# A Fourier and Hyena encoder layer on one core: the filter taps' first operations ordered behind the Fourier copies, and six second weight parts made by a GpSimd subtraction

## The chip, the cores and the metric

The kernel runs on one core of one Trainium2 chip. A core has a matrix engine (TensorE, PE in the profile, with its weight loads as PEld), VectorE (DVE), ScalarE (ACT), GpSimd (POOL) and SyncE (SP, which here only issues transfers), each with its own in-order stream of instructions, and 16 DMA engines that all queues share. The metric is the device time in microseconds of one execution, and less is better. The time of the kernel before is the median of three runs, 2421.94 us (2418.77 to 2423.49).

## What is computed

Two sequences of 1024 positions and 1024 channels go through the same layer in float32. Cut to what matters:

```python
xn = rmsnorm(x, g_pre)
p = xn @ w_in                                   # 1024 x 8192
fv, fg, hv, hg, mg = split(p)                   # 1, 1, 3, 1, 2 times 1024 columns
fz = fft2(fv in 4 groups of 256 channels).real  # over positions and a group's channels
y_f = (fz * silu(fg)) @ w_fourier_out
v, x1, x2 = split(short_conv(hv, w_short))      # width 3 along the positions
kf = hyena_filters(...)                         # rfft of filters made by a small sine network
z = v
for n, gate in enumerate((x1, x2)):
    z = gate * long_conv(z, kf[:, n], hyena_d[n])
y_h = (z * silu(hg)) @ w_hyena_out
g_f, g_h = split(sigmoid(mg + b_merge))
out = (g_f * y_f + g_h * y_h) @ w_out
return x + rmsnorm(out, g_post)
```

A filter is the product of a sine network's output (`hid` here) with a third weight matrix, times an exponential decay, divided by the sum of its absolute values. These products are called taps below.

## The kernel before

Nearly every product is made from two parts: a number is rounded to a first part h, and the rest is the second part l, so that h + l is the number. A product of two numbers is then three matmuls (h h, h l, l h; `mm3`). A helper, `split`, makes the parts: ScalarE casts to h, and an engine that is named subtracts h from the number, which gives l.

The kernel has three stages. **`phase_fourier`** norms both sequences, stores their transposes in DRAM (`d_x`) and makes the Fourier branch for each sequence in two halves (`fourier_half`). A half first multiplies with the weights (`pfv`), copies an edge column product (`x5t`, lines 411 and 412), and then runs five times a helper `stage`: matmuls with cosine and sine tables into two PSUM banks (`pse`, `pso`), a ScalarE copy of the even part (`sev`, line 434), VectorE's sum and difference into `sst`, and a split. The even stages of both channel groups are first (with results `pp`), then the one of the edges (`px`), then the odd stages (`qp`, one buffer each). Further matmuls (`pP`, `pQ`) follow, and the results `fA` and `fB` are stored to `d_fz` by transfers in GpSimd's queue. The last half that runs is the second sequence's first.

**`phase_main`** loads the first sequence back (`load_x`: eight transfers of 512 KB, each split into `xh` and `xl`), loads `hid` and rounds it (lines 915 to 917), and then goes through 16 rounds, two orders by eight channel tiles. A round makes the taps of the next filter (`filter_taps`), the spectrum of the current one (`filter_spectrum`), and one or two projections of the gate branches (`spill_gate`, through `inproj`) that fill TensorE. `filter_taps` loads a weight tile and the decay by SP's queue; on ScalarE it casts the weights (`w3s`), takes the decay's absolute value, and makes eight exponentials and four absolute values; its products (`pft`) are on TensorE, and their multiplication by the exponentials (`T`) on VectorE. Behind the rounds come the Hyena convolutions of both sequences, and then **`phase_blocks`** with the second sequence's remaining projections and the three output products.

A projection in `inproj` takes its weights in two halves of 128 x 512 numbers (256 KB). A half is loaded into a raw buffer (`wr`, two buffers) in SP's queue; ScalarE casts h. The second part is made in one of two ways. With `plain`, VectorE subtracts. Otherwise ScalarE writes -h into l (line 765), and a transfer in GpSimd's queue reads the weights from DRAM again and adds them to l on the way (line 766); it needs no engine's arithmetic beyond the negation. The parts lie in rooms that are taken in turn (`rooms`): two halves in `wh` and `wl`, then one in `draw` and one in `draw2`. `draw2` belongs to a pool of `phase_main`, and the memory of these pools is that of the Fourier stage.

The order of the work is not written out around the change. The kernel is traced with `TileContext(nc, schedule_with_timeline_sim=True)`: the builder puts each engine's instructions in an order by its own estimate of their times, so instructions of `phase_main` stand among those of the last Fourier half where it finds them ready. Only `phase_blocks` has its order written out. `tc.issue_after(i)` adds to every instruction that is traced inside it, and that runs on the engine of instruction i, the rule that it is ordered behind i; instructions on other engines get none.

Of the kernel before, what the change touches and what calls it, by code (L numbers as in the profile page):

```python
# [161 lines left out]
class K:  # L162
# [223 lines left out]
    def fourier_half(self, b, half, W, fo, px, pf, begun={}):  # L386

        nc = self.nc
# [5 lines left out]
        for e, (W_, n, X_) in enumerate(((WE, 260, EE), (WO, 256, OO))):  # L394
            for m in range(4):
# [6 lines left out]
                if e == (b + half == 0):  # L402

                    if m == 0:
                        p5 = self.psum("X", 2, "pfx")[0:36, :260]
# [2 lines left out]
                            self.mm(p5, fo["x5"][:, k], WE[i][:, k], k + i == 0, k + i == 8)  # L408

        X5, XX, PX = fo["x5t"], fo["xx"], fo["px"]  # L410
        nc.scalar.copy(X5[0:36], p5)
        self.sub("dve", X5[32:36], p5[32:36], X5[32:36])

        EX = fo["ex"]
# [8 lines left out]
        def stage(np_, data, e, edge, out, tag):  # L423

            pe = self.psum(tag, 2, "pse")[0:np_, :258]
            po = self.psum(tag, 2, "pso")[0:np_, :258]
            for m in range(4):
                last = (edge is None and m == 1) or m == 3
                self.mm3(pe if m < 2 else po, data(m), (seq[:, 0, e, m], seq[:, 1, e, m]), m % 2 == 0, last)
                if m == 1 and edge is not None:  # L430
                    self.mm(pe.rearrange("p (a b) -> p a b", a=3), edge, al, False, True)
            ev = pf.tile([P, 258], F32, tag="sev", name="sev", bufs=1)[0:np_]
            st = pf.tile([P, 514], F32, tag="sst", name="sst", bufs=1)[0:np_]
            nc.scalar.copy(ev, pe)
            self.add("dve", st[:, 0:258], ev, po)
            if e == 0:
                self.sub("dve", st[:, 512:257:-1], ev[:, 0:255], po[:, 0:255])
            else:
                self.stt("dve", st[:, 512:257:-1], ev[:, 0:255], -1.0, po[:, 0:255])
            nc.vector.tensor_copy(st[:, 513:514], st[:, 0:1])  # L440
            if len(out) == 2:
                self.split(out[0], out[1], st, "dve", "act")
            else:
                nc.scalar.copy(out[0][0:34], st)
                self.sub("dve", out[0][32:34], st[32:34], out[0][32:34])
# [3 lines left out]
        for g in range(2):  # L449
            cs = slice(130 * g, 130 * g + P)  # L450
            PP.append(pair([P, 514], "pp", 2))
            stage(P, lambda m: (EE[0][:, m, cs], EE[1][:, m, cs]), 0, X5[:, cs], PP[g], "TX"[g])
        stage(34, lambda m: (EX[0][:, m], EX[1][:, m]), 0, XX, [PX], "T")
        for g in range(2):
            Pp, Qp = PP[g], pair([P, 514], "qp")
            co = slice(P * g, P * g + P)
            stage(P, lambda m: (OO[0][:, m, co], OO[1][:, m, co]), 1, None, Qp, "XT"[g])
            A = pf.tile([P, 1026], F32, tag="fAB", name="fA", bufs=3)
            B = pf.tile([P, 1026], F32, tag="fAB", name="fB", bufs=3)
            gg = 2 * half + g  # L460
            for n in range(2):
# [17 lines left out]
                r = slice(0, w)  # L479
# [3 lines left out]
                r = slice(0, w)  # L483
# [258 lines left out]
    def inproj(self, sec, mt, b=None, plain=False):  # L742

        nc, a = self.nc, self.a
        ps = [self.psum("mm", 4, f"pin{n}") for n in range(2)]
        for q in range(2):
            s = slice(512 * q, 512 * q + 512)
            src = a["w_in"][sec, mt][:, s]
            kept = self.d_w[sec - 1][mt] if b is not None else None
            if b or plain:  # L750
                h, l = [self.wp.tile([P, 512], F32R, tag=g, name=g, bufs=2) for g in ("wh", "wl")]
            else:
                h, l = self.rooms()
            if b:
                self.keep_parts()
                for t, k in zip((h, l), kept):
                    nc.sync.dma_start(t.bitcast(F32), k[:, s])
            else:
                r = self.wp.tile([P, 512], F32, tag="w", name="wr", bufs=2)
                nc.sync.dma_start(r, src)  # L760
                if plain:
                    self.split(h, l, r, "dve", "act")
                else:
                    nc.scalar.copy(h, r)
                    nc.scalar.mul(l, h, -1.0)
                    self.added = nc.gpsimd.dma_start(l, src, accum_op=ADD)
                    self.keep_parts()
                    if kept:
                        self.unsaved = [(t, k[:, s]) for t, k in zip((h, l), kept)]
            h, l = [t.rearrange("p (a b) -> p a b", a=4) for t in (h, l)]  # L770
            for n in range(2):
                for kk in range(4):
                    k = 4 * q + kk
                    s = slice(512 * n, 512 * n + 512)
                    self.mm3(ps[n], (h[:, kk], l[:, kk]), (self.xh[k][:, s], self.xl[k][:, s]), k == 0, k == 7)
        return ps
# [127 lines left out]
    def phase_main(self, nct=8, nb=NB, nf=16):  # L904
        tc, nc, a = self.tc, self.nc, self.a
        with ExitStack() as es:
            pool = lambda n: es.enter_context(tc.tile_pool(name=n, bufs=1, reuse_waits="tile"))
            mf, wa, wb, mi = pool("mf"), pool("wa"), pool("wb"), pool("mi")
            self.stage2 = pool("m2")
            self.turn, self.unsaved = 3, []  # L910
            ws = Rooms(wa, wb)
            self.load_x(0, range(4))
            self.hid = ws.tile([P, L], F32R, tag="q", name="hid", bufs=2)
            hid = ws.tile([P, L], F32, tag="q", name="hidr", bufs=2)
            nc.sync.dma_start(hid, self.d_h)
            nc.scalar.copy(self.hid, hid)
            self.sub("dve", self.hid[64:128], hid[64:128], self.hid[64:128])
            taps = self.filter_taps(0, 0, ws)
            self.load_x(0, range(4, 8))
            self.cfw0 = mf.tile([P, 4 * P], F32, name="cfw0")  # L920
            self.cfwd = mf.tile([P, 2, 12 * P], F32R, name="cfwd")
            nc.sync.dma_start(self.cfw0, a["c_fw0"])
            nc.gpsimd.tensor_copy(self.cfwd[:, 0, 0:1], self.xl[4][:, 0:1])
            nc.gpsimd.dma_start(self.cfwd, a["c_fwd"])
            for t, n in ((self.th, "c_th"), (self.wsh, "w_short"), (self.bm, "b_merge")):
                nc.sync.dma_start(t, a[n])
            plain = [(5, c) for c in range(8)] + [(6, c) for c in range(8)] + [(4, c) for c in range(NH)]
            fill = sorted([((2 * c + 1) / len(plain), t) for c, t in enumerate(plain)]
                          + [((2 * c + 1) / max(NF, 1), (0, c)) for c in range(NF)])
            fill = [t for _, t in fill]  # L930
            for i in range(nf):
                nxt = self.filter_taps((i + 1) % 2, (i + 1) // 2, ws) if i + 1 < nf else None
                gates = fill[i * len(fill) // nf:(i + 1) * len(fill) // nf]
                if i < nf - 1:
                    self.filter_spectrum(i % 2, i // 2, taps, ws)
                for sec, c in gates:
                    self.spill_gate(0, sec, c, ws)
                if i == nf - 1:
                    first = [self.conv(1 + n, 0, ws, "vx"[n], 0, True) for n in range(2)]
                    self.filter_spectrum(i % 2, i // 2, taps, ws)  # L940
                taps = nxt
                if i == 4:
                    self.cinv = mi.tile([P, 2, INVW], F32R, name="cinv")
                if 4 <= i < 12:
                    w = slice((i - 4) * INVW // 8, (i - 3) * INVW // 8)
                    with tc.issue_after(self.added.ins):
                        nc.gpsimd.dma_start(self.cinv[:, :, w], a["c_inv"][:, :, w])
            self.branches(nb, nct, ws, *first)
# [576 lines left out]
```

## Time and profile before

| | |
|---|---|
| median of 3 runs | 2421.94 us (2418.77 to 2423.49) |
| profiled execution | 2420.15 us |
| its span | 2418.3 us |
| mean granted TensorE clock | 0.994 |
| PE busy | 2360.6 us, 98% |
| DVE busy | 1976.0 us, 82% |
| ACT busy | 1147.7 us, 47% |
| POOL busy | 447.5 us, 19% |
| DMA | 499.63 MB, 207 GB/s over the span |

The profile is of one execution. Its page gives busy time by engine, the span in slices, the DMA queues, the chain of work that ended last, and groups of equal instructions with what ended the idle time ahead of them. A timeline lists instructions with start and duration, and in brackets the idle time of the engine ahead of one and who released it; equal instructions in a row are merged, with their count. Matmuls are pipelined: one of 512 columns has a recorded duration of some 0.39 us, while the next starts 0.23 us later at the full clock. The granted clock is the share of full speed that TensorE was given.

### The profile page before, as it was taken

The page shows a single profiled execution, that of the slowest core. Times are in us where ns is not written, and L with a number is a line of the kernel's source. Part 1 is how long each engine was busy: PE and PEld are TensorE (multiplying, and loading weights), DVE is VectorE, ACT ScalarE, POOL GpSimd, SP SyncE. Part 2 cuts the span into 40 slices and gives each one's busy share as a digit, 9 for nine tenths or more (in the row PEclk, how much of TensorE's full clock was granted, in tenths as well). Part 3 has the DMA queues.
Part 4 walks back from the last instruction along what each step waited for, and adds up shares of the span by engine and source line. Part 5 has one row for each costly group of instructions (what it writes and reads, how often), then busy time and mean ns, then how long its engine had stood idle before and what let it go on. Part 6 is the DMA issues. An engine that isn't in the chain of part 4 may idle for free. (4 is left out here: it accounts for less than half of the span.)

```text
span 2418.3 us, 37119 instructions
## 1 busy us (share of the span) xinstructions
PE 2360.6 (98%) x13006; PEld 2050.7 (85%) x13006; DVE 1976.0 (82%) x3760; ACT 1147.7 (47%) x2140; POOL 447.5 (19%) x575
## 2 busy tenths in 40 slices
PE   6999899999999999999999999999999999999998
PEld 6998788888888888888888888888878888888886
DVE  7786888888737999899899999997666687777787
ACT  6546666666544444344222322333344475656543
POOL 1331111111123332221023454310000000101000
PEclk9999899999999999999999999999999999999999
DMA  7536688787778777666365666553546687888754
GB/s 277 187 127 220 179 222 222 202 225 215 202 219 254 221 223 209 192 177 200 126 194 191 210 218 205 187 179 123 205 158 230 210 298 256 267 270 230 222 159 154
DMA packets 265010, 499.63 MB, mean 207 GB/s; under 512 B 26662, under 2 KB 92423, under 8 KB 264568
## 3 DMA queue, kind: packets, MB, share of 16 engines
q1 hardware_dynamic: 220076, 380.53, 48.0%
q0 software_dynamic: 44560, 116.72, 19.0%
q8 instruction: 102, 1.67, 0.3%
q14 instruction: 84, 0.69, 0.1%
q10 hardware_dynamic: 188, 0.02, 0.0%
HBM read 333.59 MB, written 167.77 MB: 207 GB/s over the span
## 5 line engine op out<-in xcount | busy, mean ns | idle before, releaser
L194 PE MATMUL pin<-xh,wh 128*128 128x512 f32 x1024 | 401.2, 393 | 0.4 <-DMA wh<-d_w 0.4
L194 PE MATMUL pin<-xl,wh 128*128 128x512 f32 x1024 | 401.2, 392 | 0.0
L194 PE MATMUL pin<-xh,wl 128*128 128x512 f32 x1024 | 399.6, 392 | 0.0
L194 PE MATMUL pin<-xh,whl 128*128 128x512 f32 x896 | 292.4, 397 | 8.1 <-DMA whl<-in_w_in 4.5
L194 PEld LDWEIGHTS pin<-xh,wh 128*128 128x128 f32 x1024 | 192.8, 188 | 35.9 <-DMA wh<-d_w 0.8
L194 PEld LDWEIGHTS pin<-xh,wl 128*128 128x128 f32 x1024 | 192.7, 188 | 35.6 <-DMA wl<-in_w_in 0.2
L194 PEld LDWEIGHTS pin<-xl,wh 128*128 128x128 f32 x1024 | 192.7, 188 | 34.8
L194 PEld LDWEIGHTS pin<-xh,whl 128*128 128x128 f32 x896 | 168.3, 190 | 42.8 <-DMA whl<-in_w_in 5.2
L194 PE MATMUL pT<-cinv,yh 128*128 128x256 f32 x1024 | 192.9, 283 | 2.7 <-ACT yh L171 2.7
L194 PE MATMUL pin<-xl,whl 128*128 128x512 f32 x448 | 178.1, 398 | 0.0
L194 PEld LDWEIGHTS pT<-cinv,yh 128*128 128x128 f32 x1024 | 165.4, 191 | 12.9 <-ACT yh L171 3.2
L194 PE MATMUL pX<-bh,cfwd 128*128 128x256 f32 x768 | 159.3, 287 | 0.9 <-ACT bh L171 0.9
L181 DVE TENSOR_TENSOR t<-pX,k 128x1024 f32<-128x1024 f32 x128 | 155.7, 1216 | 3.9 <-PE pX L194 2.9
L171 ACT CAST yh<-y 128x512 fp32r<-128x512 f32 x128 | 79.3, 620 | 152.8 <-DVE y L181 113.1
L194 PE MATMUL pT<-cinv,yl 128*128 128x256 f32 x512 | 145.5, 284 | 0.0
L171 ACT CAST bh<-b 128x512 fp32r<-128x512 f32 x144 | 88.9, 619 | 98.3 <-DVE b L181 58.1
L194 PEld LDWEIGHTS pX<-bh,cfwd 128*128 128x128 f32 x768 | 125.8, 191 | 4.6 <-ACT bh L171 1.3
L181 POOL TENSOR_TENSOR draw<-draw 128x256 f32<-128x256 f32 x96 | 93.8, 977 | 112.1 <-DMA draw<-in_w_out 39.5
L181 DVE TENSOR_TENSOR bl<-b,bh 128x512 fp32r<-128x512 f32 x144 | 100.3, 703 | 11.5 <-ACT bh L171 11.4
L194 PE MATMUL pX<-bl,cfwd 128*128 128x256 f32 x384 | 109.5, 285 | 0.0
L181 DVE TENSOR_TENSOR yl<-y,yh 128x512 fp32r<-128x512 f32 x128 | 90.2, 705 | 16.9 <-ACT yh L171 16.5
L194 PEld LDWEIGHTS pT<-cinv,yl 128*128 128x128 f32 x512 | 98.2, 192 | 1.9
(368 smaller groups left out, 6030.0 us busy)
## 6 DMA issues: line engine op xcount, KB each, us to landing
k<-d_k SPq DMA_DIRECT2D x128, 512.0 KB, 4.6
wr<-in_w_in SPq DMA_DIRECT2D x136, 256.0 KB, 3.6
d_g<-gt SPq DMA_DIRECT2D x92, 256.0 KB, 3.3
d_k<-kt SPq DMA_DIRECT2D x128, 128.0 KB, 3.7
d_k<-kt SPq DMA_DIRECT2D x64, 256.0 KB, 3.6
fz<-d_g SPq DMA_DIRECT2D x64, 256.0 KB, 5.1
wl<-in_w_in POOLq DMA_DIRECT2D x56, 256.0 KB, 5.4
whl<-in_w_in POOLq DMA_DIRECT2D x56, 256.0 KB, 5.7
```

The source lines that it names most:

```text
L171: self.rounded = nc.scalar.copy(h, src)
L181: return e.tensor_tensor(out, a, b, op=op)
L194: return self.nc.tensor.matmul(out, lhsT, rhs, start=start, stop=stop, skip_group_check=shared)
```

## The change

Two things are changed.

In the first, the first ScalarE operations of `phase_main` are ordered behind copies of the last Fourier half. The cast of `hid` goes behind the copy of the edge product (`self.edge`, line 411), and ScalarE's part of the first `filter_taps` behind the second of the five copies of `stage` (`self.evens[1]`, line 434).

In the second, a new case is added to `inproj`: in rounds 0 and 1 (`self.opening`) the second part is made by GpSimd's subtraction from the raw buffer. That are three projections, six halves. From round 2 on it is made by negation and transfer as before.

```diff
         X5, XX, PX = fo["x5t"], fo["xx"], fo["px"]
-        nc.scalar.copy(X5[0:36], p5)
+        self.edge = nc.scalar.copy(X5[0:36], p5)
+        self.evens = []
         self.sub("dve", X5[32:36], p5[32:36], X5[32:36])
...
-            nc.scalar.copy(ev, pe)
+            self.evens.append(nc.scalar.copy(ev, pe))
             self.add("dve", st[:, 0:258], ev, po)
...
                 nc.sync.dma_start(r, src)
-                if plain:
-                    self.split(h, l, r, "dve", "act")
+                if plain or self.opening:
+                    self.split(h, l, r, "dve" if plain else "pool", "act")
                 else:
                     nc.scalar.copy(h, r)
                     nc.scalar.mul(l, h, -1.0)
...
             nc.sync.dma_start(hid, self.d_h)
-            nc.scalar.copy(self.hid, hid)
+            with tc.issue_after(self.edge.ins):
+                nc.scalar.copy(self.hid, hid)
             self.sub("dve", self.hid[64:128], hid[64:128], self.hid[64:128])
-            taps = self.filter_taps(0, 0, ws)
+            with tc.issue_after(self.evens[1].ins):
+                taps = self.filter_taps(0, 0, ws)
             self.load_x(0, range(4, 8))
...
             for i in range(nf):
+                self.opening = i < 2
                 nxt = self.filter_taps((i + 1) % 2, (i + 1) // 2, ws) if i + 1 < nf else None
```

## The prediction

> **What bounds the kernel now.** I read the page's head first, then busy time by stage.
>
> ```profile
> span 2418.3 us, 37119 instructions
> ```
>
> ```profile
> 200.00:300.00 100.00, 85.52 (x455) 72.55 (x455) 74.92 (x164) 60.50 (x121) 11.77 (x17) 0.90 0.68 204
> 300.00:1710.00 1410.00, 1403.78 (x8114) 1235.75 (x8113) 1222.51 (x2365) 618.05 (x1189) 339.97 (x420) 1.00 0.68 199
> ```
>
> The columns after each stretch are its length, then PE, PEld, DVE, ACT and POOL busy, the granted TensorE clock, the DMA share and GB/s. TensorE sets the time: between 300 and 1710 us it lacks 1410 - 1403.78 = 6.2 us. Between 200 and 300 it lacks 14.5 us at a granted clock of 0.90. What is won there reaches the end, because nothing behind it leaves TensorE free time that could swallow it. Next, that stretch in finer steps, and what ended TensorE's idle times in it (the bracket is the idle time and its releaser).
>
> ```profile
> 212.00:218.00 6.00, 5.62 (x24) 4.77 (x25) 5.22 (x11) 4.91 (x9) 0.00 (x0) 0.55 1.03 420
> ...
> 254.00:261.00 7.00, 2.30 (x18) 1.89 (x16) 6.03 (x12) 3.70 (x9) 1.06 (x2) 0.81 0.43 164
> 261.00:268.00 7.00, 2.18 (x5) 1.26 (x5) 7.00 (x15) 3.93 (x9) 1.76 (x2) 0.50 0.60 135
> ```
>
> ```profile
> 203.26 0.63 PE L194 MATMUL pQ<-qp,chan 128*128 128x256 f32 x3 [0.99 <-DVE fB L177]
> ...
> 204.08 2.08 PE L194 MATMUL pfx<-we,x 128*36 128x260 f32 x16
> ...
> 209.56 0.51 PE L194 MATMUL pse<-alt,x5t 128*128 128x258 f32 x2 [2.46 <-DVE x5t L181]
> ...
> 212.38 1.50 PE L194 MATMUL pse<-seq,ex 128*34 128x258 f32 x6 [1.50 <-ACT sev L434]
> ...
> 215.18 1.05 PE L194 MATMUL pin<-xh,wh 128*128 128x512 f32 x2
> ...
> 232.31 0.63 PE L194 MATMUL pft<-w3s,hid 128*128 128x256 f32 x4
> ...
> 256.96 0.73 PE L194 MATMUL pft<-w3s,hid 128*128 128x256 f32 x4 [1.40 <-DVE T L181]
> 261.31 0.80 PE L194 MATMUL pin<-xh,whl 128*128 128x512 f32 x1 [3.62 <-ACT whl L764]
> ...
> 262.76 0.63 PE L194 MATMUL pin<-xl,whl 128*128 128x512 f32 x1
> 267.90 1.22 PE L194 MATMUL pin<-xh,whl 128*128 128x512 f32 x2 [4.51 <-DMA whl<-in_w_in]
> ...
> 272.65 0.39 PE L194 MATMUL pin<-xl,whl 128*128 128x512 f32 x1
> ```
>
> There are two holes. The one at 203 to 215 lies in the last Fourier half; the one at 255 to 268 is the wait for one weight part. Either is followed by matmuls at half clock. The change touches a releaser of both.
>
> **First part: the first taps behind the Fourier copies.** What ScalarE did while TensorE waited:
>
> ```profile
> 205.75 1.05 ACT L916 CAST hid<-hidr 128x1024 fp32r<-128x1024 f32 x1 [1.72 <-DMA hidr<-d_h]
> 206.71 0.40 ACT L171 CAST w3s<-w 128x256 fp32r<-128x256 f32 x1
> 208.38 0.42 ACT L632 ACTIVATE dec<-dec 128x256 f32<-128x256 f32 x1 [1.27 <-DMA dec<-in_filt_decay]
> 208.70 0.35 ACT L411 CAST x5t<-pfx 36x260 fp32r<-36x260 f32 x1
> 209.07 1.28 ACT L643 ACT_TABLE_LOAD   x1
> 210.37 1.70 ACT L643 ACTIVATE ex<-dec,vec 128x256 f32<-128x256 f32 x4
> 211.98 0.35 ACT L434 COPY sev<-pse 128x258 f32<-128x258 f32 x1
> ```
>
> The pfx matmuls end at 204.08 + 2.08 = 206.16, but their copy (x5t) stands behind the hid cast, the w3s cast and the decay's absolute value, which waits for its own load, and starts at 208.70. Put ahead of them it can start at about 206.3, 2.4 us earlier; TensorE's wait of 2.46 falls to about 0.1: **-2.35**. The next copy (sev) stands behind a table load and four exponentials and starts at 211.98, though its matmuls end at 209.56 + 0.51. Only the hid cast (1.05) can now stand in front of it, from 206.65 to 207.7, while TensorE works. The wait of 1.50 goes: **-1.50**. The six matmuls that take 1.50 us at half clock (0.25 each), and the six after them, would run at the full one: 215.18 - 212.38 = 2.8 us become 12 x 0.125 and a little, 1.6, **-1.2**. Together TensorE would be through at 210.1 instead of 215.18.
>
> Next late are the activations of the first gate projections:
>
> ```profile
> L722 SPq DMA_DIRECT2D xl<-d_x x8: 326/589/1222, 204.1 to 210.8; - x8
> ...
> DMA to landing us min/median/max: 7.8/11.3/12.8
> ```
>
> The first was issued at 204.1 and takes at least 7.8 us: 211.9, and with a cast as long as hid's (1.05) 213.0. The DMA share is 1.03 there, so the loads don't come faster. So this part is worth 215.18 - 213.1 = 2.1 us if TensorE then stands idle, and up to 5.1 if the odd stage's matmuls (two times 12, 3.0 us by the same 0.125) are put into the gap. Which it is, the builder's order decides; I take 3.5, near the middle: **term A = -3.5**, between -2.1 and -5.1.
>
> What moves: the hid cast, and of the taps ScalarE's share alone, one cast, the absolute value, the table load, eight exponentials of some 0.43 and four absolute values. Their loads stay on SP, their matmuls and VectorE's operations are not pinned, though they follow what they read (the subtraction of hid, which stood ahead of x5t's on VectorE, goes behind it). The first product of the taps stands at 232.31, some 20 us behind the exponentials, so 3 to 4 us of lateness there cost nothing; if the builder drew these matmuls forward, the lateness would show as a wait for the exponentials.
>
> **Second part: the second weight parts by GpSimd.** Rounds 0 and 1 hold three gate projections, six halves of weights; I call them p0 to p5, the next p6. The transfers of the first three were issued by 193.83, far ahead of 215.18:
>
> ```profile
> 193.83 0.85 POOL L766 DMA_DIRECT2D whl<-in_w_in  x1 [0.54 <-ACT whl L765]
> 194.82 0.57 POOL L486 DMA_DIRECT2D d_fz<-fA  x1
> ```
>
> The one that counts is p3:
>
> ```profile
> 260.65 0.60 ACT L764 CAST whl<-wr 128x512 fp32r<-128x512 f32 x1
> ...
> 262.72 0.61 ACT L765 ACTIVATE whl<-whl 128x512 fp32r<-128x512 f32 x1
> ...
> 263.63 0.89 POOL L766 DMA_DIRECT2D whl<-in_w_in  x1 [6.36 <-ACT whl L765]
> ```
>
> From the cast's end at 261.25 to the matmul at 267.90 pass 6.65 us: the negation, queued behind another load's wait, the issue, and the transfer. A subtraction on GpSimd takes the place of all three. No 128x512 subtraction into this type stands in the trace; the nearest rows:
>
> ```profile
> L181 POOL TENSOR_TENSOR x<-x,sg 128x512 f32<-128x512 f32 x16 | 31.9, 2008 | 38.5 <-ACT sg L1012 38.4
> ...
> L181 POOL TENSOR_TENSOR wo<-wor,wo 128x256 fp32r<-128x256 f32 x16 | 13.9, 882 | 20.7 <-ACT wo L171 20.7
> ```
>
> That is 2 x 0.88 = 1.76 from below and 2.01 from above; I take 1.9. The part is there at 261.25 + 0.1 + 1.9 = 263.25. The four matmuls at 261.31 to 262.76, which read the first part alone, last until about 263.2, so the 4.51 us go. From 261.31 to 272.65 TensorE ran 4 + 12 = 16 matmuls in 11.34 us. The ramp behind 267.90 lasted 4.75 us; a like one from 261.31 ends at 266.0 with 11 done at 0.43 each (261.31 and 262.76 are three apart at 0.48, so 0.43 to 0.48); five more at the full clock's 0.23 end at 267.2. Gain 5.4. VectorE is full there (7.00 of 7.00), and what TensorE wants next comes from it, so I take **term B = -5.0**.
>
> The Trainium skill ("TensorE: Matmul & The Clock Gate", section on the HAM clock gate) has the array halved after an idle window of about 3.4 us and restored after a busy one. The trace agrees on the half (0.50 at 261 to 268) and shows a longer ramp, 4.75 us; by 3.4 us the gain here would be estimated at 6.1, the sum 0.7 larger.
>
> Removed besides: six negations of 0.61 on ScalarE, six issues of 0.89 on GpSimd, six reads of 256 KB. Added: 6 x 1.9 = 11.4 us on GpSimd, which was busy 11.77 of 100 us: no bound. Queued behind the subtractions on GpSimd are the stores of the Fourier results, and the weights' raw buffer stays taken 1.9 us longer. VectorE may suffer too; one operation with and without GpSimd arithmetic beside it (at 160 to 182, and at 184 to 196), and its worst single one:
>
> ```profile
> L181 DVE TENSOR_TENSOR pp<-sst,pp 128x514 fp32r<-128x514 f32 x2 | 1.8, 912 | 1.0 <-ACT pp L171 1.0
> ...
> L181 DVE TENSOR_TENSOR qp<-sst,qp 128x514 fp32r<-128x514 f32 x2 | 1.4, 690 | 0.4 <-ACT qp L171 0.4
> ```
>
> ```profile
> 173.97 1.13 DVE L181 TENSOR_TENSOR pp<-sst,pp 128x514 fp32r<-128x514 f32 x1
> ```
>
> The slowdown is 912/690, a third. Per subtraction that is 0.6 us of VectorE, and only p3's falls where it is full; term B has room for it. A rule of the Trainium skill ("SBUF — State Buffer", section "SBUF: two separate sides") is harsher: a VectorE operation with two SBUF inputs and a GpSimd one that reads SBUF exclude each other for the whole instruction. By it the full 1.9 us would be lost at p3 and the estimate of the sum would be -6.6; the third measured above is milder.
>
> **Sum.** -3.5 - 5.0 = -8.5. The profiled execution took 2420.15 us, 1.85 above its span: 2411.65. The median shown, 2421.94, lies 1.8 above that execution; against it, 2413.4.
>
> **The rivals.** *The second hole closes wholly:* if the Fourier stage's end, ahead of the gate matmuls in TensorE's order, comes earlier, p3's room may be free before TensorE runs dry. Then 1.40 + 3.62 go too, and eleven matmuls' ramp of 0.2 each, 2.2: -15.7, or 2406. For it: p3's parts can only go where its room is free, and the Fourier stage's tiles lay there before (read from the code); against: the order that TensorE follows is made anew, and the gate work that covers moves forward with it.
>
> *Most of it is eaten:* the loads bound the first hole (-2.1). The subtraction is stretched like that worst one, 1.13 for 0.69, to 3.2 us, and p3 waits 1.2 (-4.2). VectorE, full, loses 3.2 x a third = 1.0. And the raw buffer is late:
>
> ```profile
> 238.60 0.62 ACT L764 CAST wh<-wr 128x512 fp32r<-128x512 f32 x1
> ...
> 241.98 0.62 ACT L764 CAST whl<-wr 128x512 fp32r<-128x512 f32 x1 [0.43 <-DMA wr<-in_w_in]
> ```
>
> The load of p6 followed p5's cast; now it follows p5's subtraction, 1.9 us later, ScalarE stands in its queue that much longer, and the last Fourier copies behind it delay p3's room: +1.9. Three subtractions ahead of the Fourier store at 194.82 cost about 0.6 on the wait of 0.99. Sum -2.8: 2419.
>
> *Slower:* the builder orders every instruction behind the first change anew. In 300 to 1710 VectorE is busy 1222.51 of 1410, and a worse interleaving there shows as TensorE waiting for copies:
>
> ```profile
> PE pT L194 <- ACT yh L171: 2.7, 1, 2.7
> ...
> PE tph L824 <- ACT T1s L875: 2.2, 1, 2.2
> ```
>
> Six more such waits of 2.4 are 14.5 us: -8.5 + 14.5 = +6, or 2428. It decides from (8.5 + 4.8) / 2.4, five to six waits. Against it: there are 6.2 us of idle in 1410 now, so an order without such waits is the rule.
>
> **How the numbers follow.** Chances: forecast (2413) 0.45, second hole closed (2406) 0.15, eaten (2419) 0.26, slower (2428) 0.14. A measurement of this kernel tells about 0.2%, 4.8 us, from no change: faster 0.45 + 0.15 = 0.60, same 0.26, slower 0.14. The range takes in the first three with the spread of the shown runs, from 2403 to 2424; only the slower case lies outside.
>
> **What would show it.** Right: x5t's copy within 0.5 us of the pfx matmuls, no wait over 0.5 us for x5t or sev, p3's second part from a GpSimd row of 1.7 to 2.1 us, no wait for a weight transfer before 275, PE missing 5 to 7 us less between 200 and 300, and the later stretch as before. Wrong: the idle time returning in front of the first projection or p3, VectorE rows above 0.9 us beside the subtractions, or idle beyond 6.2 us between 300 and 1710.

## The result, and the profile after

The changed kernel takes **2430.14 us** (median of 21 runs, 2422.32 to 2432.74); the kernel before, in runs between them on the same chip, 2421.82 (21 runs, 2418.47 to 2425.23). The ratio is 1.0033, with a 95% interval of 1.0025 to 1.004: the change makes the kernel slower by 8.3 us. The forecast was 2413, faster; the time lies outside its range of 2403 to 2424.

The profiled execution of the changed kernel took 2426.13 us, against 2420.15 before. First the head of the page after, then its busy time by stage, with the columns of the same view in the prediction (length; PE, PEld, DVE, ACT and POOL busy; clock; DMA share; GB/s).

```profile
span 2424.3 us, 37130 instructions
```

```profile
200.00:240.00 40.00, 36.01 (x208) 31.07 (x207) 27.31 (x52) 23.31 (x42) 5.60 (x7) 0.96 0.66 239
240.00:270.00 30.00, 25.82 (x118) 20.86 (x117) 23.17 (x47) 17.55 (x38) 6.47 (x8) 0.89 0.55 157
270.00:300.00 30.00, 26.03 (x137) 22.61 (x136) 23.26 (x61) 15.90 (x34) 2.56 (x3) 0.89 0.66 174
200.00:300.00 100.00, 87.86 (x459) 74.55 (x458) 73.74 (x158) 56.77 (x113) 14.62 (x17) 0.91 0.62 195
...
430.00:500.00 70.00, 66.85 (x370) 57.16 (x370) 55.66 (x133) 47.06 (x105) 9.64 (x12) 1.00 0.76 204
...
300.00:1710.00 1410.00, 1400.47 (x8087) 1230.76 (x8086) 1223.10 (x2360) 617.03 (x1192) 341.66 (x420) 1.00 0.68 199
```

Before, the first three of these stretches and the fifth read:

```profile
200.00:240.00 40.00, 35.05 (x195) 29.95 (x195) 25.59 (x49) 23.90 (x42) 2.67 (x5) 0.91 0.72 244
240.00:270.00 30.00, 20.47 (x103) 16.83 (x102) 23.06 (x52) 17.41 (x38) 5.66 (x8) 0.81 0.61 168
270.00:300.00 30.00, 30.00 (x159) 25.78 (x159) 26.26 (x65) 19.19 (x43) 3.44 (x4) 0.97 0.70 188
...
430.00:500.00 70.00, 70.00 (x394) 61.12 (x393) 60.55 (x147) 48.47 (x106) 10.36 (x13) 1.00 0.85 230
```

So 200 to 270 is better, as forecast (36.01 + 25.82 = 61.83 us of PE, for 35.05 + 20.47 = 55.52 before). But 270 to 300, which had no gap, now lacks 4 us, and 430 to 500 lacks 3.1, where nothing was missing either. TensorE's timeline after, at the two old holes and the two new ones:

```profile
208.72 0.90 PE L194 MATMUL pso<-seq,ex 128*34 128x258 f32 x6 [0.47 <-DVE sst L441]
213.13 0.73 PE L194 MATMUL pin<-xh,wh 128*128 128x512 f32 x2 [3.52 <-ACT xh L171]
...
214.16 1.49 PE L194 MATMUL pse<-seq,oo 128*128 128x258 f32 x6
...
259.02 0.79 PE L194 MATMUL pin<-xh,whl 128*128 128x512 f32 x1 [2.51 <-ACT whl L171]
...
276.51 1.22 PE L194 MATMUL pin<-xh,whl 128*128 128x512 f32 x2 [3.97 <-DMA whl<-in_w_in]
...
280.94 0.63 PE L656 MATMUL pn<-acc,ones 128*128 128x128 f32 x2
...
435.27 0.46 PE L656 MATMUL pn<-acc,ones 128*128 128x128 f32 x2 [1.43 <-DVE acc L181]
```

The waits for x5t (2.46) and sev (1.50) are gone, and so is the one of 4.51 for p3. New are 3.52 for the first cast of the activations, 3.97 for another weight part, and 1.43 for VectorE.

Stretches of equal clock time do not hold equal work in two kernels. So I also worked out a **lag** from the traces' matmul records: at the time when the kernel before has done so many columns of matmuls, how much later (positive) the other one has done as many. The rows are single executions; "before, again" shows what two executions of one program differ by. Numbers are us.

```
time in the kernel before   200    225    240    270    300    430    500    660   1500    end
before, again               2.8    2.4    2.4    2.4    2.1    2.1    2.1    2.1    3.9    1.7
changed                     0.2   -1.4   -1.5   -7.1    1.0    0.6    5.4    5.3    7.4    6.0
changed, again              2.8    2.8    2.8   -3.1    3.4    3.4    9.3    9.2    9.2   12.1
order rules alone           3.4    1.1    1.1    1.2    1.6    1.3    0.8    1.1    3.7    2.7
subtraction alone           1.8    1.0    1.0   -4.2   -1.6    0.1    0.4    1.3    4.4    4.6
subtracted to round 2       0.9    0.6    0.6   -5.5   -1.9   -1.7   -2.1    0.0   -0.5    0.0
to round 2, no order rules -0.5   -1.1   -1.1   -6.0   -1.8   -1.1   -0.4   -0.4    1.8   -0.1
p7 subtracted too           1.7    1.3    1.3   -4.6    1.5    1.3    7.0    7.0    7.1   12.7
p7 in another room          0.8    0.7    0.6   -5.2   -1.7   -1.1   -1.0   -0.6    1.4    0.9
p3 and p7 in another room   1.4    1.3    1.3  -11.0   -4.7   -5.1   -2.0   -1.2    1.3    1.2
reloads first alone         2.6   -3.6   -3.6   -8.6   -5.6   -5.2   -5.7   -5.2   -0.2    1.2
order rules, reloads first  0.0   -6.0   -6.0  -12.7   -9.9  -10.3  -10.8  -10.3   -7.7   -7.4
change and reloads first   -0.5   -8.1   -8.1  -15.2  -11.4  -11.4  -11.7  -11.4   -8.6   -6.4
```

In the changed kernel TensorE leads by 7.1 us at 270, is 1.0 behind at 300, and 5.4 behind at 500.

### The profile page after: what moved, and what is told of

It reads as the page before. It is cut to its first block, busy times and chain, and to the rows that moved or that the text cites. A ratio compares the mean times of both kernels' runs of the same rounds, so it can differ in the third digit from the quotient of the medians.

```text
span 2424.3 us, 37130 instructions
## 1 busy us (share of the span) xinstructions
PE 2365.4 (98%) x13006; PEld 2052.2 (85%) x13006; DVE 1981.4 (82%) x3760; ACT 1141.8 (47%) x2134; POOL 452.7 (19%) x575
## 5 line engine op out<-in xcount | busy, mean ns | idle before, releaser
L194 PEld LDWEIGHTS pin<-xl,whl 128*128 128x128 f32 x448 | 86.0, 192 | 16.9
```

The source lines that it names most:

```text
L194: return self.nc.tensor.matmul(out, lhsT, rhs, start=start, stop=stop, skip_group_check=shared)
```

## The experiments

Two stories were to be told apart. In the first, the change moved one wait to the next thing in line: the activations' reload at the first hole, the weight half after next at the second. In the second, the builder's new order of all that follows is at fault, whatever the change does at the holes. A third, that GpSimd's arithmetic slows VectorE, stands among the expectations as C. Ratios are to the kernel before in the same group of runs, with 95% intervals.

### Both parts again, and each alone

The changed kernel once more; then the order rules alone (before plus the lines with `issue_after`); then the subtraction alone:

```diff
-            with tc.issue_after(self.edge.ins):
-                nc.scalar.copy(self.hid, hid)
+            nc.scalar.copy(self.hid, hid)
...
-            with tc.issue_after(self.evens[1].ins):
-                taps = self.filter_taps(0, 0, ws)
+            taps = self.filter_taps(0, 0, ws)
```

> The changed kernel once more, for a second profile. Theory H (handed over): the time won by p3's subtraction is lost again because the next weight part in the same room, p7, is still made by a transfer, and the rest of the loss stands at 430 to 490 us, where the order of the filter rounds is another. Then the same waits come back in this profile: 3.5 to 4.5 us for a weight transfer at 272 to 277, and 1 to 2 us for the sum of absolute values near 434. Theory S (scatter): the loss is that of single executions, and these waits are elsewhere or gone. Time under H 2424 to 2432.

> The order edges alone, second weight parts all by transfer as before. H: x5t and sev are copied early, but TensorE then waits 3 to 4 us for the first cast of the reloaded activations, so it leads by 1 to 2 us at 230; the wait of 4.5 us for p3's transfer is there as before; at 300 the lead is 1 to 2 us. Rounds behind it, up to where the order is that of before again (near 660), give or take 5 us: 2416 to 2425. A rival, C (contention: GpSimd's arithmetic stretches VectorE's), expects this one to be free of the loss: 2419 to 2421.

> The subtraction alone, no order edges. H: the first hole as before (2.5 and 1.5 us), p3 is made 4 to 5 us earlier, and a wait of 3 to 5 us for a weight transfer comes within 20 us behind it; at 300 TensorE is 0 to 2 us behind before. C: VectorE's subtractions of 128x512 take over 0.9 us beside GpSimd's in 254 to 300, and the loss at 300 is 3 us or more. Time under H 2420 to 2430, under C 2425 to 2432.

Measured: both parts 2428.01, ratio 1.0028 (1.0018 to 1.0038); order rules 2421.51, 1.0001 (0.9989 to 1.0012); subtraction 2426.02, 1.0015 (1.0005 to 1.0026). The result repeats, and so do its waits: in the second profile TensorE waits 3.23 us for the same weight transfer (at 279.93), 1.64 for VectorE's `gt` ahead of it (0.24 in the first; this operation reads a projection's result), and 1.1 for the sum near 434. The order rules gain nothing in the time; TensorE's waits for the first casts of the activations are 2.6 us in sum there, under the 3 to 4 expected, and the wait for p3 is 4.57, as before.

The subtraction gives 5.2 us between 240 and 270, as term B had it (1.0 to -4.2), and yet ends slower. Here one expectation failed: the next weight transfer was to cost TensorE 3 to 5 us and costs 0.9 (of its waits from 200 to 500: total, times, longest).

```profile
PE pin L194 <- DMA whl<-in_w_in: 0.9, 1, 0.9
```

What became of the first hole is in ScalarE's timeline of the changed kernel:

```profile
205.30 0.37 ACT L411 CAST x5t<-pfx 36x260 fp32r<-36x260 f32 x1 [2.17 <-PE pfx L194]
205.58 1.04 ACT L918 CAST hid<-hidr 128x1024 fp32r<-128x1024 f32 x1
206.61 0.38 ACT L435 COPY sev<-pse 128x258 f32<-128x258 f32 x1
212.03 1.04 ACT L171 CAST xh<-xl 128x1024 fp32r<-128x1024 f32 x1 [5.05 <-DMA xl<-d_x]
```

Both copies are early as forecast. Then ScalarE itself waits 5.05 us for the reload, and TensorE starts at 213.13, where the prediction had its bound of 213.0. The odd stage's matmuls did not fill the gap: they stand behind the first gate matmuls, and ran at half clock (six in 1.49 us).

### Where the second gain goes

In the changed kernel the wait at 276.51 is for the half that TensorE uses next but one after p3; counted like the others it is p7. It lies in `draw2`, as p3 does, and that room has one buffer (read from the code), so p7's cast cannot start before p3's last matmul, which starts at 267.39. ScalarE and GpSimd after:

```profile
268.35 0.60 ACT L765 CAST whl<-wr 128x512 fp32r<-128x512 f32 x1
268.99 0.63 ACT L766 ACTIVATE whl<-whl 128x512 fp32r<-128x512 f32 x1
```

```profile
237.92 1.31 POOL L181 TENSOR_TENSOR wl<-wr,wh 128x512 fp32r<-128x512 f32 x1 [7.36 <-PE pQ L194]
...
259.06 1.74 POOL L181 TENSOR_TENSOR whl<-wr,whl 128x512 fp32r<-128x512 f32 x1 [4.20 <-ACT whl L171]
...
270.15 0.85 POOL L767 DMA_DIRECT2D whl<-in_w_in  x1 [0.28 <-issue]
```

The transfer, issued at 270.15, ended the wait at 276.51. Three ways to touch it, without anything left out of the computation: subtract in round 2 too (with and without the order rules); subtract p7 alone; leave p7 its transfer, but put it, or p3 and p7, into the other room.

```diff
-                self.opening = i < 2
+                self.opening = i < 3
```

```diff
+                self.nth = getattr(self, "nth", -1) + 1
-                if plain or self.opening:
+                if plain or self.opening or self.nth == 7:
```

```diff
+        self.nth = getattr(self, "nth", -1) + 1
-        if n < 2:
+        if n < 2 or self.nth in (7,):       # (3, 7) in the second version
```

> The changed kernel with the subtraction in round 2 as well (two projections more, p6 to p9, p7 among them). H: no wait over 1 us for a weight transfer before 290, and TensorE leads before by 5 to 7 us at 290; behind it the rounds' order gives or takes up to 5 us: 2412 to 2425, some 6 us under the changed kernel. C: four subtractions more make it slower than the changed kernel by 1 to 3 us.

> The subtraction in rounds 0 to 2 without the order edges. H: p3's gain of 4 to 5 us, of which VectorE, busy without a break at 255 to 275, takes back 2 to 3 by 300; the edges are worth under 2 us, so the time is that of the variant with edges, 2419 to 2424. A rival E (the edges do harm, by bringing the exponentials later): 3 us or more under it, 2416 to 2419.

> The changed kernel with one weight half more, p7, made by the subtraction; the orders of VectorE and SyncE are the changed kernel's, TensorE's differs in eleven places. Theory H: the wait of 3.5 to 4.2 us for a weight transfer at 272 to 277 goes, with it most of VectorE's stop of 6.6 us, so VectorE comes to 300 us less than 3 us behind the kernel before (5.6 in the changed kernel), and TensorE's waits at 430 to 495, 5 us in sum, fall under 2: 2419 to 2424, 5 to 9 us under the changed kernel. Rival O (order alone): with the same order the waits at 430 to 495 stay at 4 to 6 us, and the time falls by 0 to 4 us.

> The changed kernel with p7 put into a room of the other pair (wh and wl) instead of draw2, so that it can be made while p3 is still in use; it is made by a transfer as in the changed kernel. Theory R (the room's turn): the stop at 268 to 277 goes, 5 us of waits and 2 to 3 us of half clock, VectorE comes to 300 with no more than 3 us of delay, and the waits at 430 to 495 go with the delay: 2420 to 2424. Rival O (the rounds' order, whatever the delay): the stop goes, but VectorE's delay or waits of 3 us or more come back in the rounds; 2425 to 2430.

> The changed kernel with both p3 and p7 in the other pair of rooms. If p3's first wait (2.5 us) is for the memory that the Fourier stage gives back, it goes too, with its ramp: TensorE leads before by 8 us or more at 270, and the time is 2412 to 2419. If the wait is for something else it stays, and the time is that of the variant with p7 alone moved.

> The kernel before once more, for a second profile: how far two executions of one program lie apart in the stretches 0 to 200, 200 to 660 and behind. The waits of 2.5 and 1.5 us in the first hole and of 3.6 and 4.5 us for p3 come back within 0.5 us; the first 200 us and the part behind 660 differ by up to 3 us each.

Measured: to round 2, 2422.45, 1.0005 (0.9991 to 1.002); the same without order rules 2424.01, 1.0013 (1.0 to 1.0026); p7 subtracted too 2429.92, 1.0027 (1.0014 to 1.004); p7 in the other room 2420.5, 0.9997 (0.9987 to 1.0007); p3 and p7 there 2422.32, 1.0007 (0.9997 to 1.0018). The kernel before gave 2421.81 in its one further execution, which is the lag table's measure of scatter; its waits in the two holes came back as 2.25, 0.74, 3.62 and 4.47 us, so the one for sev (1.50 in the first profile) was not within the 0.5 us expected.

With p7 alone in the other room the whole loss is gone. TensorE's waits from 215 to 500 in that kernel (total, times, longest):

```profile
PE pn L656 <- DVE acc L181: 2.7, 1, 2.7
PE pin L194 <- ACT whl L171: 2.5, 1, 2.5
PE pft L194 <- DVE db L181: 1.2, 1, 1.2
PE pft L194 <- DVE T L181: 0.2, 1, 0.2
PE pXf L194 <- ACT gt L810: 0.2, 1, 0.2
```

No weight transfer is waited for, and nothing at 430 to 500. But it is no faster than before, either. What stands first is a wait of 2.7 us for VectorE, 10 us behind p3's first matmul; with subtraction to round 2 it is one of 2.9 for VectorE's `gt` at the same place:

```profile
PE pin L194 <- DVE gt L177: 2.9, 1, 2.9
```

So when neither p3 nor p7 is waited for, TensorE runs into VectorE; the lead of 5 to 7 us at 290 that was expected with subtraction to round 2 is not there (1.9 at 300). Part of VectorE's lateness is the subtraction's own doing. Between p3's subtraction and the waited-for operation VectorE runs practically without a gap, and beside that subtraction one of its operations takes 1.77 us instead of 0.68; this is the row with p7 in the other room:

```profile
261.21 1.77 DVE L181 TENSOR_TENSOR fE<-T 128x512 f32<-128x512 f32 x1
```

That is 1.1 of the 2.7 us. With subtraction to round 2 there are two such rows ahead of `gt` (1.76 and 1.78), 2.2 of the 2.9. No run takes p3's wait away without GpSimd's arithmetic beside VectorE, so how much of these waits would be left without it is not shown.

p7 subtracted too would have to be as good, if the transfer alone were late. It is not (2419 to 2424 was expected), and the trace shows one reason. GpSimd and VectorE in that kernel:

```profile
272.01 5.84 POOL L181 TENSOR_TENSOR whl<-wr,whl 128x512 fp32r<-128x512 f32 x1
```

```profile
271.68 0.75 DVE L181 TENSOR_TENSOR b<-bs 128x256 f32<-128x256 f32 x2
272.36 0.81 DVE L181 TENSOR_TENSOR b<-xp 128x256 f32<-128x256 f32 x3
273.10 1.22 DVE L177 SCALAR_TENSOR_TENSOR b<-bs,xm 128x128 f32<-128x128 f32 x5
274.24 0.28 DVE L181 TENSOR_TENSOR acc<-acc 128x128 f32<-128x128 f32 x1
274.44 0.48 DVE L177 SCALAR_TENSOR_TENSOR b<-bs,xm 128x128 f32<-128x128 f32 x2
274.85 0.68 DVE L177 SCALAR_TENSOR_TENSOR gt<-gt,fz 128x512 f32<-128x512 f32 x1
275.45 1.28 DVE L181 TENSOR_TENSOR bl<-b,bh 128x512 fp32r<-128x512 f32 x2
276.65 0.59 DVE L177 SCALAR_TENSOR_TENSOR kt<-pXf,th,ktmp 128x128 f32<-128x128 f32 x2
```

One subtraction lasted 5.84 us and ended at 277.85, while VectorE ran without a gap on operands in SBUF. The last of these ended at 276.73, and 1.1 us later the subtraction was done; `kt`, which reads PSUM (`pXf`), did not hold it up. TensorE waited 2.89 us for it at 277.91. So this kernel does not test the transfer by itself: it replaces the transfer's lateness by a starved subtraction. The rival story, order alone, had expected the idle time of 4 to 6 us at 430 to 495 to stay in it, and 3.9 us of it did (430 to 500); this kernel does not decide between the two.

The version with both in the other room is of use too. TensorE leads by 11.0 us at 270 there, since p3's earlier wait of 2.51 goes as well, as was expected if that wait is for the Fourier stage's memory. The time expected from it, 2412 to 2419, did not come. A new wait of 4.4 us for a transferred `wl`, with half clock behind it (granted clock 0.54 from 286 to 293), takes the lead from 13.0 us at 292 to 4.7 at 300, and one of 1.7 us for a taps' sum at 472 takes 3.1 more between 430 and 500:

```profile
PE pin L194 <- DMA wl<-in_w_in: 4.4, 1, 4.4
...
PE pn L656 <- DVE acc L181: 1.7, 1, 1.7
```

### The reload first

The first hole's bound is tested by having SyncE issue the first four reloads ahead of the loads of `hid` and of the taps; with the order rules alone, with the kernel before, and with the whole change.

```diff
-            nc.sync.dma_start(r, self.d_x[b][k])
+            self.xload = nc.sync.dma_start(r, self.d_x[b][k])
...
-            self.hid = ws.tile([P, L], F32R, tag="q", name="hid", bufs=2)
...
+            with tc.issue_after(self.xload.ins):
+                self.hid = ws.tile([P, L], F32R, tag="q", name="hid", bufs=2)
...
```

> The order edges alone, and SyncE issues the first four reloads of the activations ahead of the load of hid and the taps' loads. If the first hole is bounded by the reload (term A), the first cast of it starts 2 to 3 us earlier behind the pfx matmuls, TensorE's wait for it falls from 2.6 us to under 1, and TensorE's lead at 230 grows from 2 to some 4 us: 2416 to 2421. If not, the wait stays, or an equal one for the taps' loads takes its place: 2419 to 2424.

> Kernel before, with SyncE's order alone changed: four reloads of the activations ahead of hid's and the taps' loads; no order edges on ScalarE, no subtraction. If the reloads' place in SyncE's queue was what bounded the first hole, and hid and the taps, loaded later, then come behind the Fourier copies by themselves, this is as fast as with the edges: 2414 to 2419. If the edges are needed, 2419 to 2423.

> The changed kernel as it is (edges and subtraction), with the four reloads first in SyncE's queue. If the subtraction's gain (p3, 4 to 5 us) adds to that of the reloads, 2410 to 2414; theory R expects it to be lost again within 40 us, so that it is no faster than the variant without the subtraction: 2416 to 2424.

Measured: order rules with the reload first 2416.05, 0.9975 (0.9962 to 0.9989); reload first alone 2415.25, 0.9975 (0.9964 to 0.9987); the whole change with it **2412.91**, 0.9967 (0.9954 to 0.998), faster than both kernels, by 7.7 us against before. The reload alone was profiled in its slowest run (2421.1), so its last column in the lag table is not its median. SyncE's row in the changed kernel, then its rows with the order rules, reload first, and ScalarE's first cast there:

```profile
204.38 6.74 SPq L723 DMA_DIRECT2D xl<-d_x  x8
```

```profile
201.34 6.33 SPq L723 DMA_DIRECT2D xl<-d_x  x4
207.71 1.14 SPq L917 DMA_DIRECT2D hidr<-d_h  x1
```

```profile
209.34 1.05 ACT L171 CAST xh<-xl 128x1024 fp32r<-128x1024 f32 x1
```

The first reload is issued at 201.34, not 204.38, the cast starts at 209.34, not 212.03, and the wait for it is gone: 6.0 us are won up to 225. The cast now follows ScalarE's copy `sev` and waits for no load. The reloads also land sooner behind their issue: the fastest recorded in 4.7 us, against 7.6 in the changed kernel. So the reload did bound the first hole. The same 6.2 us are won without the order rules. There the Fourier copies are early by themselves: `hid`, loaded later, is cast only at 219.86, and x5t's copy waits for TensorE alone:

```profile
208.74 0.37 ACT L411 CAST x5t<-pfx 36x260 fp32r<-36x260 f32 x1 [2.14 <-PE pfx L194]
```

So the order of the loads does the work of the order rules as well; that the copies on ScalarE do not matter is not shown. TensorE's waits from 200 to 500 in the best kernel:

```profile
PE pin L194 <- DVE gt L177: 2.7, 1, 2.7
PE pin L194 <- ACT whl L171: 2.1, 1, 2.1
PE pft L194 <- DVE T L181: 0.4, 1, 0.4
PE pin L194 <- POOL whl L181: 0.2, 1, 0.2
```

Again VectorE is what TensorE runs into behind p3 (at 261.48). p7 is still made by a transfer here and is not waited for. So at both holes the first story holds: the wait moved to what stood next in line. But how long p7 is waited for depends on the order too, 3.97 and 3.23 us in the changed kernel, 0.9 with the subtraction alone and none here, and each of these versions has an order of its own. The first story had expected 2416 to 2424 for the best kernel, and its time lies below that; but whether the change still adds something to the reload (2412.91 against 2415.25) lies within the intervals.

## Why the prediction was wrong, point by point

**"What is won there reaches the end, because nothing behind it leaves TensorE free time that could swallow it."** This step failed. It looked for free time in the kernel before, where TensorE had none because it was itself the late one. Leading by 7.1 us at 270, it is no longer: the next weight half and VectorE's results are then the late ones. All 7.1 us are gone by 300, in the wait for p7 and the half clock behind it. In the versions in which p7 is not waited for (p7 in the other room, subtraction to round 2), 3.5 and 3.6 us of the 5.8 and 6.1 won from 240 to 270 are given back by 300, with the waits of 2.7 and 2.9 for VectorE. The step failed for the gain at p3, and not for every gain: with the reload first alone, TensorE leads by 3.6 us at 225 and still by 5.2 at 660.

**Term A (-3.5).** Its copies moved as worked out, and the bound by the reload (start at 213.0) was right to 0.1 us. The mistake is the value taken between the ends, near the middle: the gap was not filled, and TensorE idled 3.52 us, with half clock from 214.15 to 217.57. From 200 to 240 the changed kernel won 1.7 us, its repeat 0.0, and the order rules alone 2.3. In the four further versions with the order rules and the reload in its old place (to round 2, p7 too, and the two with other rooms) it is 0.1 to 0.4; the kernel before differs from itself by 0.4. The term is 0 to -2.3, at or outside the low end of its own bounds, -2.1 to -5.1; what a new idle time does to the clock was left out of the lower one. "The loads don't come faster" held for this change, which does not move them, and not once they were issued first (4.7 us above).

**Term B (-5.0).** Right in size: -5.6 from 240 to 270, -5.9 in the repeat, -5.2 with the subtraction alone. Its subtraction took 1.74 us against 1.9 priced. The failure is in what comes next. I asked what p3 waited for and not who uses its room after it. p7's chain of cast, negation, issue and transfer (268.35 to 276.51) is of the same kind as the one that was removed and hangs on p3's last matmul. Its wait of 3.97 us and the half clock behind it, to 282.42, make up most of the 8.1 us given back from 270 to 300 (6.5 in the repeat). VectorE stood still meanwhile, as its timeline shows:

```profile
274.57 0.68 DVE L177 SCALAR_TENSOR_TENSOR gt<-gt,pin 128x512 f32<-128x512 f32 x1
281.83 0.17 DVE L658 RECIPROCAL invn<-pn 128x1 f32<-128x1 f32 x1 [6.58 <-PE pn L657]
```

The sum of the taps (`pn`) stands behind p7's matmuls in TensorE's order, so VectorE, which was 4.71 us busy of 5 from 276 to 281 before, did nothing for 6.58 us.

**The second loss.** From 430 to 500 another 4.8 us go (5.9 in the repeat), 3.1 of them as the idle time in the stage's row above, in waits for VectorE and for ScalarE behind it; the one for the sum `acc` at 435.27 is the longest. Between the end of such a sum and TensorE's use of it lay 2.5 and 2.7 us in two rounds here before, and 0.2 and 0.1 now; the sums end 5.5 and 5.6 us later than before (410.11 and 435.13). That would fit VectorE's stop at 276. But with the subtraction alone the same two sums are 5.3 and 5.0 us later than before and 0.2 and 0.1 us ahead of their use, and from 430 to 500 TensorE is idle for only 0.5 us. So lateness of these sums does not by itself make the loss; the orders differ in all these kernels, and its cause stays open.

**The rivals.** "Slower" had 0.14 and was right in sign. Its mechanism was not: the order of instructions is the same as before again from about 660 us on, and TensorE's idle time in 300 to 1710 grew from 6.2 to 9.5 us, not by six waits of 2.4, nearly all of it at 430 to 500. "Second hole closed" came true in one version (p3 and p7 in the other room): 12.3 us are won there from 240 to 270, some 7 more than in the changed kernel, but nothing of it is left at the end. "Eaten" had the loads as bound, which was right, but priced them as a smaller gain. Of the prediction's own signs of being wrong three came: the idle time in front of the first projection (3.52), a VectorE row of 1.76 beside a subtraction, and idle time beyond 6.2 us between 300 and 1710.

**What stays open.** The profiles of the changed kernel end 6.0 and 12.1 behind; the holes account for 5.2 and 6.5 of that by 500, from 200 on. Beyond 660 lags still drift by up to 6 us from one execution to the next, in the best kernel too. And the subtraction alone, with a wait of only 0.9 for p7, loses 5.4 us in the median, of which its one trace places 2.9 between 300 and 660 and 3.3 behind. Neither is explained. So it is shown how the gain at p3 is lost by 300, and not why the kernel then ends 8.3 us slower; with p7 in the other room all of that is gone, but in another order of instructions.

## What to carry to other kernels

Before a removed wait is counted as gain, ask which buffer the stage hands on, who waits for that buffer, and how far ahead the next engine is: here VectorE took back 3.5 of the 5.8 us won at p3 even where no buffer was waited for. If a transfer bounds a stage, look first at what is issued ahead of it: the order of a few loads was worth 5.4 us alone, while the work on the two waits was worth nothing by itself.

## What the runs showed of the hardware

**GpSimd and VectorE exclude each other.** I had priced a slowdown of a third. It was the mean of two rows, one of 0.70 us that ran free and one of 1.13 that was held up, and so no price of any single operation. In the changed kernel GpSimd's subtraction lasts 1.31 us at 237.92 and 1.74 at 259.06 (rows above). VectorE beside the second:

```profile
258.98 0.68 DVE L181 TENSOR_TENSOR fO<-T 128x512 f32<-128x512 f32 x1
259.58 1.76 DVE L181 TENSOR_TENSOR fE<-T 128x512 f32<-128x512 f32 x1
261.27 0.68 DVE L181 TENSOR_TENSOR T<-pft,ex 128x512 f32<-128x512 f32 x1
```

`fO` runs first, and the subtraction ends 1.14 us after it (260.80). `fE`, which takes 0.68 otherwise, ends 0.54 after that. So each waited for the other's whole operation. This is the rule of the Trainium skill ("SBUF — State Buffer", section "SBUF: two separate sides"), an exclusive lock and no sharing, which the prediction set aside as harsher than its row; the trace agrees with the rule, at a price of 1.08 us of VectorE here, not the full 1.9. The 5.84 us above show the other direction: there GpSimd waited under an unbroken run of such VectorE operations, and a subtraction of 4.41 us in the version to round 2 without order rules is a second case. At 259.66 it got its turn between two of them all the same; what decides this is not shown. The prediction's upper row of 2.01 for a GpSimd operation of this size is a mean as well: its 16 rows in the kernel before run from 1.29 to 4.41 us.

**Half clock.** In the changed kernel the granted clock was 0.5 from 258.53 to 265.35, from 214.15 to 217.57 and from 275.59 to 282.42, about the idle times of 2.51, 3.52 and 3.97 us. It does not always set in with the first matmul: behind the 3.52 us, which end at 213.13, four ran before it did. Behind the last, ten matmuls took 276.51 to 280.94, 4.43 us, where ten at 0.23 make 2.3: 2.1 us more, about half of the wait on top of it.
